# Fetching spilled results earlier, and making two of a pair's four weight sums by DMAs that add in place

## The chip, the cores and the metric

The kernel runs on one core of one Trainium2 chip. Its time is measured on the device, in microseconds (us). The engines that matter are TensorE (PE, the matmuls), VectorE (DVE), ScalarE (ACT), GpSimd (POOL, which here only issues DMAs) and SyncE (SP, which issues most DMAs).

## What is computed

Two layers of an encoder on 256 positions of 2048 channels, in float32. Cut to what matters here:

```python
h = rmsnorm(x, norm_w)
proj = h @ w_in          # q_m k_m v_m z_m o_m g_m q_r k_r v_r z_r gate_m gate_r
h_m = mlstm_scan(forward) + flip(mlstm_scan(backward))
u_m = head_rmsnorm(sigmoid(o_m) * h_m) * silu(z_m)
h_r = retention_scan(forward) + flip(retention_scan(backward))
u_r = head_rmsnorm(h_r) * silu(z_r)
mix = sigmoid(concat([gate_m, gate_r]) + b_mix)
y = mix[:, :2048] * (u_m @ w_proj_m) + mix[:, 2048:] * (u_r @ w_proj_r)
x = x + y @ w_out
```

After the second layer stands one more rmsnorm.

## The kernel before

Positions lie in two tiles of 128, contracted channels in 16 tiles of 128. A weight block is 2048 x 512. It is loaded from HBM in eight chunks of 128 x 1024 float32 (two contraction tiles side by side, 512 KB), each into a tile `raw` out of seven. To keep float32 accuracy every operand is split into a rounded part and a rest: ACT casts `raw` to `whi` (line 262), DVE subtracts to get `wlo` (line 263), and PE makes three matmuls for each product (lines 271 to 273: hi x hi, hi x lo of the weight, lo of the activation x hi). Twelve tiles hold `whi` and `wlo`, so at most six chunks are split ahead of PE.

`gemm` multiplies one block with both position tiles: 12 matmuls of 512 columns for each of its eight chunks. GEMMs follow one another in the order of the layer: qk, v_m (vm), q and k of the retention (qr), v_r (vr), z_m (zm), proj_m (pj), z_r (zr), proj_r (pj), w_out (wo).

Seven pairs of blocks (two of o_m, two of gate_m, one of z_r, two of gate_r) are not multiplied by `gemm`, but by `seven`, which needs seven half-size products for a pair of blocks in place of eight (the scheme of Strassen and Winograd, with four sums of weights). Its steps are items in a list with weights, and `gemm` runs as many of them behind each chunk as a running goal allows (`side_chunk`): "side work". For a column chunk i (0 to 3) of a pair, `p1` loads three chunks of weights, r11, r12 and r22, and multiplies r11; `p5` makes r11 + r12 (line 268, through `wsum`) and multiplies it; `p6` adds r22 to that, into the tile `keep` (line 445), and multiplies; `p7` makes r12 + r22 (line 268) and multiplies. After all four i, `middle` combines the products to one result, and `p2` to `p4` go over the lower half: two loads r21 and r22, products of each, and `p4`, which adds r21 to `keep` (line 268) and multiplies. `end` makes the other three results. So a column chunk has four sums on DVE, 56 of each kind in the whole run (7 pairs, 4 chunks, 2 layers).

Results that are needed later (hm, om, gm, hr, zr, gr, ym, y, x: 128 x 512 float32, 256 KB) go to HBM by `spill` (a DMA on POOL's queue, line 99) and come back by `fetch` (a DMA on SP's queue, line 105) into tiles of 512 columns, of which there are seven. `gated` is such a step beside the zm GEMMs: it fetches hm_b and so_b (the spilled hm and om), multiplies them on DVE and squares them on ACT.

Steps that run beside a GEMM are generators in a list `pending`; `run_later` advances the first of them by one `yield` behind each chunk, from chunk number `lead` on (3 unless given). The order of instructions on each engine is made by a scheduler from the order of the code and from priorities: `tc.high_priority(offset=n)` moves an instruction n instructions ahead of its place (AHEAD is 800, URGENT 1600), and `vec` and `sca` are DVE and ACT with URGENT (their rows all have line 119). Every engine and every queue takes its instructions in that order.

## Time and profile before

| what | value |
|---|---|
| median of three runs | 2194.8 us (2194.19 to 5458.12) |
| the profiled execution's own time | 2194.46 us |
| its span, first to last instruction | 2192.4 us |
| mean granted TensorE clock | 0.995 |
| PE busy | 2154.0 us, 98% |
| DVE busy | 1813.4 us, 83% |
| ACT busy | 1304.3 us, 59% |
| POOL busy | 66.9 us, 3% |
| moved by DMA | 518.25 MB, 236 GB/s on average |

Busy time is the union of an engine's instructions; a matmul's end is modelled, and matmuls overlap, so a busy PE can still be short of work for some tenths of a us at a time. The 5458.12 us is a single run far off the other two and is not used.

### The profile page before, as it was taken

Reading aid. Unit: us, or ns where it says so; the run is one execution under the profiler, and the core shown is the slowest. Engines: PE = TensorE matmul, PEld = TensorE weight load, DVE = VectorE, ACT = ScalarE, POOL = GpSimd, SP = SyncE. Lnnn points to the kernel's source line nnn. Section 1 sums busy time; section 2 is a strip of 40 time slices with the busy share of each in tenths; the row PEclk is TensorE's granted clock in tenths of the full one; section 3 lists DMA queues with packets and bytes.
Section 4 is the critical chain, followed back from the end, with each engine's and each line's share of the span. In section 5 each row is a group of like instructions: output and inputs, shape, how many; then the busy total and the mean of one; then the engine's idle time right before and its main releaser. Section 6 shows DMA issues by size and latency. Waiting matters only on the chain.

```text
span 2192.4 us, 28486 instructions
## 1 busy us (share of the span) xinstructions
PE 2154.0 (98%) x10024; PEld 1809.9 (83%) x10024; DVE 1813.4 (83%) x2327; ACT 1304.3 (59%) x1627; POOL 66.9 (3%) x130
## 2 busy tenths in 40 slices
PE   7999999999999999999999999999999999999998
PEld 7988888888778888888899888888887788888887
DVE  6997898897898998985578778989978989889854
ACT  6745466656775656564457555665567656565543
POOL 0000000000000000000000000000000000000000
PEclk9999999999999999999999999999999999999999
DMA  8645577767777887887656456776777778878963
GB/s 277 213 150 190 191 236 236 229 229 241 241 241 264 280 283 258 271 295 276 221 168 208 164 185 210 236 234 216 240 247 239 255 255 292 280 252 277 326 223 125
DMA packets 161071, 518.25 MB, mean 236 GB/s; under 512 B 19616, under 2 KB 22176, under 8 KB 160928
## 3 DMA queue, kind: packets, MB, share of 16 engines
q1 hardware_dynamic: 143552, 471.98, 65.4%
q0 software_dynamic: 9600, 31.46, 3.6%
q10 hardware_dynamic: 7776, 13.00, 2.0%
q8 instruction: 78, 1.28, 0.2%
q14 instruction: 65, 0.53, 0.1%
HBM read 482.81 MB, written 33.55 MB: 236 GB/s over the span
## 4 chain that ended last, share of the span: by engine, by line
issue 48%; PE 42%; DVE 3%; DMA 3%; POOL 2%; ACT 1%; SPq 0%; ACTq 0%; POOLq 0%; DVEq 0%
PE pj L272 3%; PE pj L273 3%; PE pj L271 3%; DVE wlo L263 2%; PE vm L271 1%; PE vm L272 1%; PE wo L273 1%; PE wo L272 1%; PE wo L271 1%; PE vr L271 1%; PE vr L272 1%; PE qr L271 1%; PE vm L273 1%; PE qr L273 1%; PE vr L273 1%
## 5 line engine op out<-in xcount | busy, mean ns | idle before, releaser
L262 ACT CAST whi<-raw 128x1024 fp32r<-128x1024 f32 (+2 forms) x832 | 844.6, 1034 | 608.1 <-DVE raw L268 147.7
L263 DVE TENSOR_TENSOR wlo<-raw,whi 128x1024 fp32r<-128x1024 f32 (+2 forms) x832 | 981.0, 1200 | 214.7 <-ACT whi L262 200.1
L272 PE MATMUL pj<-wlo,u_hi 128*128 128x512 f32 x512 | 199.4, 390 | 0.6 <-DVE wlo L263 0.5
L271 PE MATMUL pj<-whi,u_hi 128*128 128x512 f32 x512 | 199.9, 391 | 0.0
L273 PE MATMUL pj<-whi,u_lo 128*128 128x512 f32 x512 | 199.3, 389 | 0.0
L262 ACT CAST whi<-keep 128x1024 fp32r<-128x1024 f32 x112 | 117.7, 1051 | 60.0 <-PE qr L272 12.8
L263 DVE TENSOR_TENSOR wlo<-keep,whi 128x1024 fp32r<-128x1024 f32 x112 | 136.4, 1218 | 15.7 <-ACT whi L262 15.1
L268 DVE TENSOR_TENSOR raw<-raw 128x1024 f32<-128x1024 f32 x112 | 136.4, 1218 | 0.8
L271 PE MATMUL qk<-whi,ht_hi 128*128 128x384 f32 (+2 forms) x320 | 113.7, 357 | 10.5 <-ACT whi L262 10.5
L272 PE MATMUL qk<-wlo,ht_hi 128*128 128x384 f32 (+2 forms) x320 | 113.4, 354 | 1.0 <-DVE wlo L263 1.0
L272 PEld LDWEIGHTS pj<-wlo,u_hi 128*128 128x128 f32 x512 | 96.1, 188 | 21.0 <-DVE wlo L263 1.5
L273 PE MATMUL qk<-whi,ht_lo 128*128 128x384 f32 (+2 forms) x320 | 113.0, 353 | 0.0
L273 PEld LDWEIGHTS pj<-whi,u_lo 128*128 128x128 f32 x512 | 96.1, 188 | 20.0
L271 PEld LDWEIGHTS pj<-whi,u_hi 128*128 128x128 f32 x512 | 96.0, 188 | 20.0 <-ACT whi L262 0.4
L272 PE MATMUL zm<-wlo,ht_hi 128*128 128x512 f32 x256 | 100.0, 391 | 1.0 <-DVE wlo L263 0.9
L271 PE MATMUL vm<-whi,ht_hi 128*128 128x512 f32 x256 | 100.3, 392 | 0.0
L273 PE MATMUL vm<-whi,ht_lo 128*128 128x512 f32 x256 | 100.2, 391 | 0.0
L271 PE MATMUL vr<-whi,ht_hi 128*128 128x512 f32 x256 | 100.1, 391 | 0.0
L271 PE MATMUL qr<-whi,ht_hi 128*128 128x512 f32 x256 | 100.1, 391 | 0.0
L272 PE MATMUL vm<-wlo,ht_hi 128*128 128x512 f32 x256 | 100.0, 391 | 0.0
L271 PE MATMUL zm<-whi,ht_hi 128*128 128x512 f32 x256 | 100.0, 392 | 0.0
L272 PE MATMUL vr<-wlo,ht_hi 128*128 128x512 f32 x256 | 99.8, 390 | 0.0
(313 smaller groups left out, 4664.6 us busy)
## 6 DMA issues: line engine op xcount, KB each, us to landing
raw<-in_w_main_dram SPq DMA_DIRECT2D x776, 512.0 KB, 5.0
raw<-in_w_qk_dram SPq DMA_DIRECT2D x48, 384.0 KB, 3.2
bm<-in_b_mix_dram ACTq DMA_DIRECT2D x32, 256.0 KB, 4.4
raw<-in_w_qk_dram SPq DMA_DIRECT2D x15, 400.0 KB, 5.2
hm<-hm POOLq DMA_DIRECT2D x16, 256.0 KB, 4.6
om<-c POOLq DMA_DIRECT2D x16, 256.0 KB, 3.5
hr<-hr POOLq DMA_DIRECT2D x16, 256.0 KB, 5.7
gm<-c POOLq DMA_DIRECT2D x16, 256.0 KB, 4.7
```

What stands on the lines that cost most here:

```text
L262: nc.scalar.copy(out=whi, in_=raw)
L263: nc.vector.tensor_tensor(out=wlo, in0=raw, in1=whi.bitcast(F32), op=ALU.subtract)
L268: nc.vector.tensor_tensor(out=dst, in0=a, in1=b, op=ALU.add)
L271: nc.tensor.matmul(out=ps, lhsT=xh, rhs=whi, start=first, stop=False)
L272: nc.tensor.matmul(out=ps, lhsT=xh, rhs=wlo, start=False, stop=False)
L273: nc.tensor.matmul(out=ps, lhsT=xl, rhs=whi, start=False, stop=last)
```

## The change

Five edits, most of them in `seven`. `p1` loads its third chunk into a tile named t3 and then issues a DMA on POOL's queue (line 439 of the changed kernel) that adds r12 to it from HBM in place, so that t3 is r12 + r22. `p5` writes r11 + r12 over r12 and not over r11, `p6` adds r11 and t3 into `keep` (line 449), and `p7` multiplies t3 without a sum. After `p6` a second DMA on POOL's queue (line 452) adds r21 to `keep` from HBM, and `p4` loses its sum. The weights of the items p7 and p4 fall from 1.6 to 0.5. The bias rows `bm` are loaded by `early` in the last chunk of each half, on SP's queue in place of ACT's.

The fetches move: `gated` fetches all four tiles of a block at once and then pauses two slots, and the zm GEMMs run their later-steps from chunk 1 on; gm_b is fetched before its GEMM; `ur_chunk` fetches z_b like `gated`; ym_b (for b below 2) and gr_b (from 2 on) are fetched before their GEMM.

```diff
@@ -408,7 +408,7 @@
             yield
         side_start(make_items(s_hi=s_hi, s_lo=s_lo, keep=bigt("keep", 4)), 20 * NCK)
 
-    def seven(l, xop, s_hi, s_lo, keep, blk, finish):
+    def seven(l, xop, s_hi, s_lo, keep, blk, finish, early):
 
         def sop(i, kt):
             o = (i * HK + kt) * P
@@ -430,24 +430,29 @@
             if i == 0:
                 for name in "abcd":
                     st["ps_" + name] = bank("s" + name)
+            if i == HC - 1:
+                early(1)
             load("r11", 0, i)
             load("r12", 1, i)
-            load("r22", 1, HC + i)
+            load("t3", 1, HC + i)
+            with tc.high_priority(offset=AHEAD):
+                nc.gpsimd.dma_start(out=st["t3"], in_=wmain(l, blk + 1)(i), accum_op=ALU.add)
             product(st["ps_a"], lambda kt: xop(0, kt), st["r11"], i, True, True)
 
         def p5(i):
-            wsum(st["r11"], st["r11"], st["r12"])
-            product(st["ps_c"], lambda kt: sop(0, kt), st["r11"], i, True, True)
+            wsum(st["r12"], st["r11"], st["r12"])
+            product(st["ps_c"], lambda kt: sop(0, kt), st["r12"], i, True, True)
 
         def p6(i):
             with tc.high_priority(offset=AHEAD):
                 t2 = keep[:, i * CW:(i + 1) * CW]
-                nc.vector.tensor_tensor(out=t2, in0=st["r11"], in1=st["r22"], op=ALU.add)
+                nc.vector.tensor_tensor(out=t2, in0=st["r11"], in1=st["t3"], op=ALU.add)
             product(st["ps_b"], lambda kt: sop(1, kt), t2, i, True, True)
+            with tc.high_priority(offset=AHEAD):
+                nc.gpsimd.dma_start(out=t2, in_=wmain(l, blk)(HC + i), accum_op=ALU.add)
 
         def p7(i):
-            wsum(st["r12"], st["r12"], st["r22"])
-            product(st["ps_d"], lambda kt: sop(2, kt), st["r12"], i, True, True)
+            product(st["ps_d"], lambda kt: sop(2, kt), st["t3"], i, True, True)
 
         def middle():
             with tc.high_priority(offset=URGENT):
@@ -465,6 +470,8 @@
             if i == 0:
                 for name in "acd":
                     st["ps_" + name] = bank("r" + name)
+            if i == HC - 1:
+                early(0)
             load("r21", 0, HC + i)
             load("r22", 1, HC + i)
             product(st["ps_a"], lambda kt: xop(0, HK + kt), st["r21"], i, True, True)
@@ -474,7 +481,6 @@
 
         def p4(i):
             t2 = keep[:, i * CW:(i + 1) * CW]
-            wsum(t2, t2, st["r21"])
             product(st["ps_d"], lambda kt: xop(1, HK + kt), t2, i, True, True)
 
         def end():
@@ -490,11 +496,11 @@
 
         items = []
         for i in range(HC):
-            for w, fn in ((0.5, p1), (1.6, p5), (1.6, p6), (1.6, p7)):
+            for w, fn in ((0.5, p1), (1.6, p5), (1.6, p6), (0.5, p7)):
                 items.append((w, lambda fn=fn, i=i: fn(i)))
         items.append((2.0, middle))
         for i in range(HC):
-            for w, fn in ((0.5, p2), (0.5, p3), (1.6, p4)):
+            for w, fn in ((0.5, p2), (0.5, p3), (0.5, p4)):
                 items.append((w, lambda fn=fn, i=i: fn(i)))
         items.append((1.5, end))
         return items
@@ -818,25 +824,30 @@
 
         def side_items(l=l, xop=xop, rs=rs, s_hi=None, s_lo=None, keep=None):
             def finish_with(kind, b0):
+                bms = {}
+
+                def early(n):
+                    if kind in ("gm", "gr"):
+                        bms[n] = row("bm")
+                        mc = (0 if kind == "gm" else D) + (b0 + n) * NB
+                        nc.sync.dma_start(out=bms[n], in_=b_mix[l:l + 1, mc:mc + NB].broadcast_to([P, NB]))
+
                 def finish(t, n, src, own):
                     sg = t512(kind) if own is None else own
                     b = b0 + n
                     if kind in ("om", "zr"):
                         sca.activation(out=sg, in_=src, func=AF.Sigmoid if kind == "om" else AF.Silu, scale=rs[t])
                     else:
-                        bm = row("bm")
-                        mc = (0 if kind == "gm" else D) + b * NB
-                        with tc.high_priority(offset=AHEAD):
-                            nc.scalar.dma_start(out=bm, in_=b_mix[l:l + 1, mc:mc + NB].broadcast_to([P, NB]))
+                        bm = bms[n]
                         vec.scalar_tensor_tensor(out=sg, in0=src, scalar=rs[t], in1=bm, op0=ALU.mult,
                                                        op1=ALU.add)
                         sca.activation(out=sg, in_=sg, func=AF.Sigmoid)
                     spill((kind, l, b, t), sg)
-                return finish
+                return finish, early
             items = []
             for kind, base, b in (("om", B_O_M, 0), ("om", B_O_M, 2), ("gm", B_GATE, 0), ("gm", B_GATE, 2),
                                   ("zr", B_Z_R, 0), ("gr", B_GATE + NBLK, 0), ("gr", B_GATE + NBLK, 2)):
-                items += seven(l, xop, s_hi, s_lo, keep, base + b, finish_with(kind, b))
+                items += seven(l, xop, s_hi, s_lo, keep, base + b, *finish_with(kind, b))
             return items
 
         for b in range(NBLK):
@@ -892,9 +903,10 @@
         um = []
 
         def gated(h, hs, ss):
-            for t in range(NT):
-                hv = fetch(("hm", l, h, t), "hm_b")
-                so = fetch(("om", l, h, t), "so_b")
+            ops = [(fetch(("hm", l, h, t), "hm_b"), fetch(("om", l, h, t), "so_b")) for t in range(NT)]
+            yield from pause(2)
+            for t in range(NT):
+                hv, so = ops[t]
                 vec.tensor_tensor(out=hv, in0=hv, in1=so, op=ALU.mult)
                 sca.activation(out=so, in_=hv, func=AF.Square, accum_out=ss[:, t:t + 1])
                 hs.append(hv)
@@ -912,7 +924,7 @@
             hs = []
             ss_m = sm.tile([P, NT], F32, name="ss_m")
             later(gated, b, hs, ss_m)
-            ps = gemm(xop, wmain(l, B_Z_M + b), "zm")
+            ps = gemm(xop, wmain(l, B_Z_M + b), "zm", lead=1)
             while len(hs) <= NT:
                 run_later()
             rstd_m = hs[NT]
@@ -931,10 +943,12 @@
 
         uop = lambda t, kt: in_acts(um)(t, kt)
         for b in range(NBLK):
+            for t in range(NT):
+                side_need(("gm", l, b, t))
+            sgs = [fetch(("gm", l, b, t), "gm_b", 60) for t in range(NT)]
             ps = gemm(uop, wmain(l, B_PROJ_M + b), "pj")
             for t in range(NT):
-                side_need(("gm", l, b, t))
-                sg = fetch(("gm", l, b, t), "gm_b")
+                sg = sgs[t]
                 vec.tensor_tensor(out=sg, in0=ps[t], in1=sg, op=ALU.mult)
                 spill(("ym", l, b, t), sg)
 
@@ -943,16 +957,18 @@
         def ur_chunk(b, zs):
             ev = []
             hrs = [fetch(("hr", l, 2 * b + k), "hr_b") for k in range(2)]
-            for t in range(NT):
-                z = fetch(("zr", l, b, t), "z_b") if zs is None else zs[t]
+            if zs is None:
+                zs = [fetch(("zr", l, b, t), "z_b") for t in range(NT)]
+                yield from pause(2)
+            for t in range(NT):
+                z = zs[t]
                 for k in range(2):
                     i = t * NH_R + 2 * b + k
                     zk = z[:, k * S:(k + 1) * S]
                     vec.scalar_tensor_tensor(out=zk, in0=hrs[k][:, t * S:(t + 1) * S], scalar=rstd_r[:, i:i + 1],
                                              in1=zk, op0=ALU.mult, op1=ALU.mult)
                 ev.append(z)
-            if zs is None:
-                yield
+            yield
             ur[b] = transpose_split(ev, b, None, None, (l, V_RN))
             yield
 
@@ -987,12 +1003,18 @@
                 y_hi, y_lo = bigt("y_hi", 2, F32R), bigt("y_lo", 3, F32R)
                 later(y_chunk, None, 0)
                 later(y_chunk, None, 1)
+            early = []
+            for t in range(NT):
+                if b < 2:
+                    early.append(fetch(("ym", l, b, t), "ym_b", 60))
+                    continue
+                early.append(fetch(("gr", l, b, t), "gr_b", 60))
             ps = gemm(rop, wmain(l, B_PROJ_R + b), "pj", lead=2)
             ev = []
             for t in range(NT):
                 side_need(("gr", l, b, t))
-                sg = fetch(("gr", l, b, t), "gr_b")
-                ym = fetch(("ym", l, b, t), "ym_b")
+                sg = fetch(("gr", l, b, t), "gr_b") if b < 2 else early[t]
+                ym = fetch(("ym", l, b, t), "ym_b") if b >= 2 else early[t]
                 vec.tensor_tensor(out=sg, in0=ps[t], in1=sg, op=ALU.mult)
                 vec.tensor_tensor(out=sg, in0=ym, in1=sg, op=ALU.add)
                 ev.append(sg)
```

The order of instructions changes with it. Three places:

DVE, the second pair of o_m, its first column chunk. Here raw_4119 is r11, raw_4121 is r12 and raw_4123 is r22 before and t3 now; keep_2236 is `keep`. Before:

```order
L263 TENSOR_TENSOR wlo_4126<-raw_4119,whi_4125 128x1024
L119 TENSOR_TENSOR c21_4084<-rd_3783,u7_3752 128x512
L263 TENSOR_TENSOR wlo_4152<-raw_4149,whi_4151 128x1024
L268 TENSOR_TENSOR raw_4119<-raw_4119,raw_4121 128x1024
L445 TENSOR_TENSOR keep_2236<-raw_4119,raw_4123 128x1024
L263 TENSOR_TENSOR wlo_4169<-raw_4119,whi_4168 128x1024
L263 TENSOR_TENSOR wlo_4181<-raw_4178,whi_4180 128x1024
L263 TENSOR_TENSOR wlo_4198<-keep_2236,whi_4197 128x1024
L263 TENSOR_TENSOR wlo_4210<-raw_4207,whi_4209 128x1024
L119 TENSOR_TENSOR qr_lo_4032<-tr_4135,qr_hi_4031 128x512
L119 TENSOR_TENSOR qr_lo_4032<-tr_4142,qr_hi_4031 128x512
L268 TENSOR_TENSOR raw_4121<-raw_4121,raw_4123 128x1024
```

Now, from the split that frees the tile of raw_4121 (wlo_3969) over the one that frees the tile of raw_4123 (wlo_3999) to the add into keep:

```order
L263 TENSOR_TENSOR wlo_3969<-raw_3966,whi_3968 128x1024
L263 TENSOR_TENSOR wlo_3985<-keep_2236,whi_3984 128x1024
L263 TENSOR_TENSOR wlo_3999<-raw_3994,whi_3998 128x1024
L268 TENSOR_TENSOR raw_4121<-raw_4119,raw_4121 128x1024
L263 TENSOR_TENSOR wlo_4009<-raw_3996,whi_4008 128x1024
L263 TENSOR_TENSOR wlo_4039<-raw_4036,whi_4038 128x1024
L263 TENSOR_TENSOR wlo_4055<-keep_2236,whi_4054 128x1024
L119 SCALAR_TENSOR_TENSOR ca_4018<-qr0_3695,rstd_328,cos_sb_103 128x512
L119 SCALAR_TENSOR_TENSOR sa_4019<-qr0_3695,rstd_328,sin_sb_104 128x512
L449 TENSOR_TENSOR keep_2236<-raw_4119,raw_4123 128x1024
```

The sum of r12 and the add into keep stood next to each other and behind the split of r11; now both stand ahead of r11's split (which follows twelve rows later), with three splits and two other rows between them.

DVE, the second block of `gated` in layer 0: the rows from the z rows of the first block (they read its hm_b) to the second product of the second. c11 to c21 are the results of a pair of gate_m, u_lo is the split of u. Before:

```order
L119 SCALAR_TENSOR_TENSOR z_5045<-hm_b_5022,rstd_m_5034,z_5045 128x512
L119 SCALAR_TENSOR_TENSOR z_5048<-hm_b_5028,rstd_m_5034,z_5048 128x512
L263 TENSOR_TENSOR wlo_5221<-raw_5218,whi_5220 128x1024
L119 SCALAR_TENSOR_TENSOR c21_5074<-c21_5074,rstd_328,bm_5090 128x512
L119 SCALAR_TENSOR_TENSOR u_lo_5175<-tr_5176,vec_sb_101,u_hi_5174 128x256
L119 SCALAR_TENSOR_TENSOR u_lo_5175<-tr_5185,vec_sb_101,u_hi_5174 128x256
L119 TENSOR_TENSOR hm_b_5212<-hm_b_5212,so_b_5214 128x512
L119 TENSOR_TENSOR hm_b_5263<-hm_b_5263,so_b_5265 128x512
L119 SCALAR_TENSOR_TENSOR u_lo_5175<-tr_5176,vec_sb_101,u_hi_5174 128x256
L119 SCALAR_TENSOR_TENSOR u_lo_5175<-tr_5185,vec_sb_101,u_hi_5174 128x256
L263 TENSOR_TENSOR wlo_5238<-raw_5102,whi_5237 128x1024
```

Now:

```order
L119 SCALAR_TENSOR_TENSOR z_5050<-hm_b_4956,rstd_m_5036,z_5050 128x512
L119 SCALAR_TENSOR_TENSOR z_5047<-hm_b_4952,rstd_m_5036,z_5047 128x512
L119 SCALAR_TENSOR_TENSOR c11_5074<-c11_5074,rstd_328,bm_4978 128x512
L119 SCALAR_TENSOR_TENSOR c12_5075<-c12_5075,rstd_328,bm_4519 128x512
L119 SCALAR_TENSOR_TENSOR c21_5076<-c21_5076,rstd_328,bm_4978 128x512
L263 TENSOR_TENSOR wlo_5179<-raw_5136,whi_5178 128x1024
L119 TENSOR_TENSOR hm_b_5151<-hm_b_5151,so_b_5153 128x512
L268 TENSOR_TENSOR raw_5250<-raw_5248,raw_5250 128x1024
L119 SCALAR_TENSOR_TENSOR u_lo_5093<-tr_5094,vec_sb_101,u_hi_5092 128x256
L119 SCALAR_TENSOR_TENSOR u_lo_5093<-tr_5103,vec_sb_101,u_hi_5092 128x256
L119 TENSOR_TENSOR hm_b_5155<-hm_b_5155,so_b_5157 128x512
L263 TENSOR_TENSOR wlo_5191<-raw_5188,whi_5190 128x1024
```

The products moved by a row or two; three rows c stand between z and the first product where one stood, and the sum of r12 stands between the two products.

POOL, the second pair of o_m beside the retention's spills (hr). Before:

```order
L99 DMA om_0_0_1_3113<-c21_3102 128x512
L99 DMA hr_0_0_3259<-hr_3254 128x512
L99 DMA hr_0_1_3324<-hr_3319 128x512
L99 DMA hr_0_2_3606<-hr_3601 128x512
L99 DMA hr_0_3_3655<-hr_3650 128x512
L99 DMA om_0_3_1_3761<-c22_3754 128x512
L99 DMA om_0_2_0_4089<-c11_4082 128x512
L99 DMA om_0_3_0_4092<-c12_4083 128x512
L99 DMA om_0_2_1_4095<-c21_4084 128x512
```

Now:

```order
L439 DMA raw_3295<-in_w_main_dram 128x1024
L452 DMA keep_2236<-in_w_main_dram 128x1024
L99 DMA hr_0_0_3249<-hr_3244 128x512
L439 DMA raw_3445<-in_w_main_dram 128x1024
L452 DMA keep_2236<-in_w_main_dram 128x1024
L99 DMA hr_0_1_3326<-hr_3321 128x512
L439 DMA raw_3617<-in_w_main_dram 128x1024
L452 DMA keep_2236<-in_w_main_dram 128x1024
L99 DMA hr_0_2_3593<-hr_3588 128x512
```

An accumulation into t3 (raw) and one into keep now stand between two spills, and t3 of the next chunk ahead of keep of this one.

## Rows read from the trace of the kernel before

**Rows 1.** The page, part 1: busy time, share, instructions of each engine.

```profile
PE 2154.0 (98%) x10024; PEld 1809.9 (83%) x10024; DVE 1813.4 (83%) x2327; ACT 1304.3 (59%) x1627; POOL 66.9 (3%) x130
```

**Rows 2.** Timeline of PE, 573.3 to 580.5: start, length, engine, line, idle before.

```profile
573.62 0.39 PE L273 MATMUL zm<-whi,ht_lo 128*128 128x512 f32 x1
573.85 0.39 PE L271 MATMUL sd<-whi,s_hi 128*128 128x512 f32 x1
578.85 0.79 PE L272 MATMUL sd<-wlo,s_hi 128*128 128x512 f32 x1 [4.61 <-DVE wlo L263]
579.44 0.63 PE L273 MATMUL sd<-whi,s_lo 128*128 128x512 f32 x1
579.87 0.63 PE L271 MATMUL sd<-whi,s_hi 128*128 128x512 f32 x1
```

**Rows 3.** Table of stretches: length, busy of each engine, clock, DMA share, GB/s.

```profile
0.00:55.00 55.00, 43.46 (x217) 41.27 (x218) 34.68 (x77) 36.86 (x66) 1.68 (x10) 0.94 0.80 276
...
220.00:990.00 770.00, 762.65 (x3472) 633.08 (x3471) 674.01 (x730) 473.12 (x556) 27.13 (x50) 1.00 0.75 250
550.00:660.00 110.00, 102.92 (x457) 83.98 (x457) 95.77 (x131) 79.81 (x108) 2.71 (x5) 0.97 0.73 243
...
1330.00:2090.00 760.00, 752.06 (x3427) 622.11 (x3426) 666.55 (x726) 468.13 (x551) 26.05 (x48) 1.00 0.77 257
1650.00:1760.00 110.00, 102.72 (x454) 82.19 (x452) 97.12 (x127) 78.00 (x100) 3.25 (x6) 1.00 0.74 247
...
2145.00:2192.40 47.40, 38.96 (x218) 34.04 (x216) 18.58 (x37) 13.49 (x25) 0.00 (x0) 0.95 0.29 104
```

**Rows 4.** View of waits, whole run: engine, releaser, us, times, longest.

```profile
DVE wlo L263 <- ACT whi L262: 215.2, 189, 4.9
...
ACT whi L262 <- PE vm L272: 84.7, 49, 5.9
...
DVE keep L268 <- DMA raw<-in_w_main_dram: 34.0, 21, 5.1
...
DVE hm_b L119 <- DMA so_b<-om: 19.4, 11, 3.3
...
DVE c L119 <- DMA bm<-in_b_mix_dram: 8.2, 2, 4.3
...
DVE z L119 <- DMA hr_b<-hr: 7.3, 4, 2.1
...
DVE gm_b L119 <- DMA gm_b<-gm: 5.7, 2, 2.9
```

**Rows 5.** Timeline of DVE, 563.3 to 579.

```profile
569.12 0.75 DVE L119 SCALAR_TENSOR_TENSOR c<-c,rstd,bm 128x512 f32<-128x512 f32 x1
...
573.37 0.69 DVE L119 TENSOR_TENSOR hm_b<-hm_b,so_b 128x512 f32<-128x512 f32 x1 [2.72 <-DMA so_b<-om]
576.18 0.69 DVE L119 TENSOR_TENSOR hm_b<-hm_b,so_b 128x512 f32<-128x512 f32 x1 [2.12 <-DMA so_b<-om]
...
577.58 1.21 DVE L263 TENSOR_TENSOR wlo<-raw,whi 128x1024 fp32r<-128x1024 f32 x1
```

**Rows 6.** Groups of instructions of DVE by shape: count, busy, mean ns.

```profile
L268 DVE TENSOR_TENSOR raw<-raw 128x1024 f32<-128x1024 f32 x112 | 136.4, 1218 | 0.8
```

**Rows 7.** Timeline of DVE, 710 to 720: four splits in a row.

```profile
712.29 4.63 DVE L263 TENSOR_TENSOR wlo<-raw,whi 128x1024 fp32r<-128x1024 f32 x4 [1.19 <-ACT whi L262]
```

**Rows 8.** DMA view: queues, then issues with KB and us to landing.

```profile
q1 hardware_dynamic: 143552, 471.98, 65.4%
...
raw<-in_w_main_dram SPq DMA_DIRECT2D x776, 512.0 KB, 5.0
...
hm<-hm POOLq DMA_DIRECT2D x16, 256.0 KB, 4.6
...
so_b<-om SPq DMA_DIRECT2D x16, 256.0 KB, 6.1
```

**Rows 9.** Groups of instructions of POOL.

```profile
L99 POOL DMA_DIRECT2D hm<-hm x16 | 8.8, 552 | 440.4 <-ACT hm L119 440.2 <-ACT cos_sb L210 0.2
```

## Prediction

> **What bounds the kernel now.** I read the busy times first. TensorE (PE) is busy in 2154.0 of 2192.4 us, VectorE (DVE) in 1813.4 [rows 1]. A busy PE is not proof that it gives work without a break, so the timeline is next: each 512-column matmul is shown as 0.39 us long, but the next one starts 0.23 us later (573.62, 573.85) [rows 2]. The 0.23 is the pace of a fed PE. Right behind it stands a break: the next matmul starts at 578.85, and for a while afterwards the pace is 0.43 us (579.44, 579.87). The granted clock in 550:660 has a mean of 0.97, so some 3.3 us more are lost after that wait at the lower of the two levels (1.2 in place of 2.4 GHz) [rows 3].
>
> The table of stretches says where the 38.4 us lie in which PE isn't busy (2192.4 less 2154.0): 11.5 in the first 55 us, 8.4 in the last 47.4, 7.1 in 550:660 and 7.3 in 1650:1760 [rows 3]. The middle has 18.4 in all, 14.4 of them in those two stretches, which are the same place of the two layers (the z_m GEMMs). With the 3.3 us of clock, 21.7 us is everything that the change can touch; start and end are outside of it. That is 1.0% of 2194.46 us, and about 2% is what a measurement of this kernel can tell from no change.
>
> Who makes PE wait there? The wait at 578.85 ended with DVE's split (line 263) [rows 2]. DVE had come to it late: two products hm_b*so_b stood ahead of it, each held by the landing of so_b, 2.72 and 2.12 us [rows 5]. In the whole run DVE waits 19.4 us for so_b, 8.2 for bm, 7.3 for hr_b, 5.7 for gm_b, and 34.0 us for weights at the sum into keep (line 268, 21 times); the 215.2 us behind ScalarE's cast I count as room, since that cast itself often waits for PE to free a pair of split tiles (84.7 us behind the vm GEMMs alone) [rows 4]. So DVE is the second limit: in the two side stretches (220:990, 1330:2090), where the pairs' products run beside the GEMMs, it is busy 674.0 of 770 and 666.6 of 760 us and idle 96.0 + 93.5 = 189.5 [rows 3].
>
> **The change part by part.**
>
> *Two sums leave DVE.* The sums in p7 and p4 go, 56 each (4 column chunks, 7 pairs, 2 layers). One is shown as 1.218 us, but four splits in a row take 4.63 us, so one costs DVE 1.157 [rows 6, 7]. 112 x 1.157 = 129.6 us of DVE time are removed, and the 34.0 us of waits at p4's sum with them. PE gains nothing from this by itself: it is room.
>
> *Fetches ahead.* hm_b/so_b are asked for two slots earlier, gm_b before its GEMM, bm a chunk earlier and on SP instead of ScalarE. A slot holds 12 matmuls of a GEMM, 12 x 0.23 = 2.7 us, and about one side product of 6, so two slots are some 8 us, against 6.1 us that so_b takes from issue to landing [rows 8]. By that the waits named above (19.4 + 8.2 + 7.3 + 5.7 = 40.6) should go. But a fetch also needs a tile. The one that made PE wait is the second block's in both layers, and there hm_b_5151 and so_b_5153 lie, in the new program, in the tiles that hm_b_4956 and hm_b_4952 had: their fetch waits for the two z rows that read these last. From the second z to the first product stand three rows c and one split, 3 x 0.7 + 1.2 = 3.3 us [rows 5, 7], against a landing of 6.1: DVE waits 2.8 us, as before (2.72) [rows 5]. Between the two products it now has a sum and two rows u_lo, some 2 us, that before came elsewhere, so of the second wait (2.12) little should be left. So in that block I count on half, in the other three on most. The bm DMAs on SP, and the fetches that wait there for a tile, hold the weight loads behind them; seven loads are on the way by then, and that covers it as long as the wait stays below two chunks (5.4 us).
>
> *112 accumulating DMAs on POOL.* A POOL DMA occupies the engine for 0.55 us [rows 9], 62 us in all on an engine that is otherwise 3% busy [rows 1]: nothing. While such a DMA waits on POOL (t3's for its load, keep's for the split that reads the tile), the spills behind it wait too, for a load of 5 us or so; their fetches come tens of us later, so only the tiles that they free are late. For the 16 DMA engines each is at least another 512 KB load; the SP queue moved 471.98 MB in 65.4% of the span, so one load takes 1.59 us of all engines, 112 take 178 us, or 356 if the add reads both operands at that price [rows 8]. The side stretches show a DMA share of 0.75 and 0.77 [rows 3]; 178 to 356 us over 1530 make that 0.88 to 1.00. The lower end is hidden, the upper one isn't.
>
> *Two new waits on DVE.* Here is the cost that decides. In the new order the sum of r12 no longer overwrites r11, so it stands as soon as its load is expected, and the add into keep stands as soon as the accumulated t3 is expected. DVE takes its work in order: while it waits for one of these, ready splits queue behind it, and PE waits for those. In the place shown, the tile of r12 is freed by split 3969 and its sum follows two splits later: 2.3 us, where a load takes 5.0 from issue to landing [rows 8]. t3's tile is freed by split 3999; until the add into keep there are four such rows and two of 0.75 us [rows 5], 6.1 us in all, for a load and an accumulation behind each other. I counted this for all 56 pairs, with the durations of [rows 7] and a load of 5.1 us. The r12 sums: short in 44 of 56 pairs, 115 us together. The same counting for the old sum into keep gives 33 us over 26 of 56, where the trace has 34.0 over 21 [rows 4], so I trust it. The adds depend on X, the time from issue to landing of an accumulation, which no row shows. A plain 512 KB load lands in 5.0 us and is the lower bound; the upper bound is two of them in series, 10 us; 256 KB written from POOL land in 4.6 [rows 8]. I take 6.6, the load and 1.6 us for the second operand, nearest to the load's row. The adds then wait 94 us in all at X = 5.0, 168 at 6.6, 208 at 7.4, 238 at 8 and 348 at 10.
>
> The Trainium skill, page "DMA: Bandwidth & Descriptors", section "Anatomy of one DMA", fits a DMA issued from GpSimd as 2.0 us and the bytes at 436 GB/s. For 512 KB that is an estimate of 3.2 us, by which the adds would wait 22 us in place of 168; the row of plain loads, 5.0, doesn't support it for SP's queue, and no row shows one of 512 KB on POOL's.
>
> *The sum for DVE.* Room: 189.5 idle + 129.6 removed = 319 us. New waits at X = 6.6: 115 + 168 = 283. It fits, with 36 us to spare, but only as an average. Before, the waits and the sums together were 129.6 + 34.0 + 40.6 = 204; now it is 283, so DVE isn't freed, it has changed one load for another. In a z_m stretch of 110 us: 9.7 us of so_b waits go (half of 19.4) and 9.3 us of sums (64.8 x 110/770); 20.2 us of new waits come (141.5 x 110/770). That is even. What speaks for a gain in spite of it: the old waits came together (2.72, 2.12 and a GEMM's end within 10 us), the new ones are spread over the pairs, and the add stands 5 to 26 rows of DVE ahead of the split that PE needs. Of the 21.7 us the second block has 4.6 and 3.3 of clock here, and about 4.6 in the other layer (where the mean clock is 1.00): 12.5, of which half goes with the second product's wait, 6.3. The other 9.2 are gaps that I let stay, since DVE's account is even. 3 us come for places where a new wait meets a PE without a lead: 2194.5 - 6.3 + 3 = **2191 us**. Span and the time around it differ by 2.1 us (2194.46 less 2192.4), the median of the runs is 2194.8; I predict against the 2194.46.
>
> **The rivals.**
>
> *DVE blocks on the accumulations (slower).* Same place, the add into keep, with a later landing. The room of 319 less 115 is 204 us, which is X = 7.4: from there on DVE cannot do its work in the side stretches, and PE waits for each missing us. X = 8 gives 353 us of waits, 34 over the room: 2191 + 34 = 2225. X = 10 gives 463, 144 over: 2335. For it: a DMA share that goes to 0.88 or more slows loads too, and the shortfalls are in nearly every pair. Against it: DVE's idle time behind the cast shows that it usually has a lead over PE.
> The skill, same page, section "Queues, rings and completion order", says that a DMA engine takes turns between its queues packet by packet; by that a load beside an accumulation would lose up to the 1.6 us of one transfer, and if all 44 short r12 sums lost that, it would be 70 us more, 36 of which the spare room takes: 2191 + 34 = 2225 again. No row shows what such an overlap costs.
>
> *The accumulations land early.* At X = 4.6, the row of POOL's 256 KB, the adds wait 76 us, all new waits are 191, 13 us less than the 204 that go, and 18.4 + 3.3 us are won but for 2: 2175. For it: that row itself, should the second half of the bytes cost little. The skill's fit above lies on this side.
>
> *The fetches aren't earlier.* The 512-column tiles have seven buffers; four are now asked for at once by a block's hm_b and so_b, two by gm_b or gr_b, three by a pair's results. If SP has to wait for a tile in all blocks as it does in the second, the fetches land as late as now and the weights behind them as well: the change then does not do what it says, and with the DVE account even the time is 2195. For it: the second block. Against it: in the third and fourth block the tiles that the new program gives to the first product come free before the z rows of the block ahead.
>
> **How the numbers follow.** The forecast 0.40 (2185 to 2197 by itself), DVE blocked 0.37, early 0.15, no earlier fetch 0.08. Of the 0.37 I put 0.12 beyond 2% (2238, X near 8.25) and 0.25 below. Slower by over 2%: 0.12; faster by over 2%: 0.01, since all that can be won is 21.7 us; within: 0.87. The range goes from 2172 (all of the 21.7 but the last us) to 2234 (X near 8.2), which leaves some 0.13 above and 0.04 below.
>
> **What the changed profile would show.** PE without a wait of several us in 550:660 and 1650:1760, and a granted clock of 1.00 there: fetches right; one near 3 us at the second block's products: the tile rule above. DVE's waits: the row hm_b <- so_b gone or under 5 us, and new rows for raw (r12's sum) near 115 us and keep (the add) near 170 behind a DMA; if the latter is under 80, the early rival, if over 210, the slow one. The DMA view gives X directly. I'd be wrong above all if X is far from 6.6, or if PE in the z_m stretches doesn't stand a wait of 5 us of DVE at once.

## The result, and the profile after

The changed kernel takes 2446.32 us (median of 4 runs), the kernel before 2194.49: 1.1153 times as long, 95% interval 1.1131 to 1.1175 (the one run of 5458.12 us is left out of the ratio). The forecast was 2191 us, 2172 to 2234. The time lies 212 us above the range.

The page of the profiled execution (2447.13 us, span 2445.4, granted clock 0.960), part 1, answers to [rows 1]:

```profile
PE 2234.1 (91%) x10024; PEld 1850.7 (76%) x10024; DVE 1686.7 (69%) x2215; ACT 1293.7 (53%) x1621; POOL 166.8 (7%) x242
```

PE is without work for 211.3 us (2445.4 less 2234.1) where it was 38.4, and it is busy 80.1 us longer for the same 10024 matmuls, which goes with the lower clock (0.960 after 0.995). 172.9 + 80.1 = 253.0, the whole difference of the spans. DVE does 126.7 us less work, as two sums of four should give, and yet it is idle 758.7 us in place of 379.0.

The view of waits over the whole run, which answers to [rows 4] (engine, line, what it waited for; us in total, times, longest):

```profile
DVE keep L449 <- DMA raw<-in_w_main_dram: 301.7, 51, 9.7
POOL keep L452 <- DVE wlo L263: 256.2, 45, 16.1
...
DVE wlo L263 <- ACT whi L262: 197.4, 177, 4.2
ACT whi L262 <- DMA raw<-in_w_main_dram: 178.0, 59, 9.7
...
DVE raw L268 <- DMA raw<-in_w_main_dram: 126.5, 44, 6.5
...
PE pj L272 <- DVE wlo L263: 66.1, 20, 8.5
```

Two rows are new on DVE: 301.7 us at the add into keep (line 449) and 126.5 us at the sum of r12, 428.2 together; the 34.0 us at the old sum into keep are gone. The wait behind ScalarE's cast is there as before, 197.4 after 215.2. ScalarE's own wait for weights was smaller before:

```profile
ACT whi L262 <- DMA raw<-in_w_main_dram: 34.2, 21, 5.0
```

So DVE's account closes: +394.2 at the sums, -17.8 at the cast, -126.7 of work, which is 249.7 of the 253.0 us.

One such place in DVE's timeline, from 229 us on (start, length, engine and line, idle before it and what ended that):

```profile
229.19 1.21 DVE L263 TENSOR_TENSOR wlo<-raw,whi 128x1024 fp32r<-128x1024 f32 x1
232.50 1.23 DVE L268 TENSOR_TENSOR raw<-raw 128x1024 f32<-128x1024 f32 x1 [2.10 <-DMA raw<-in_w_main_dram]
233.64 2.35 DVE L263 TENSOR_TENSOR wlo<-raw,whi 128x1024 fp32r<-128x1024 f32 x2
244.56 1.23 DVE L449 TENSOR_TENSOR keep<-raw 128x1024 f32<-128x1024 f32 x1 [8.56 <-DMA raw<-in_w_main_dram]
245.70 1.22 DVE L263 TENSOR_TENSOR wlo<-keep,whi 128x1024 fp32r<-128x1024 f32 x1
246.84 4.62 DVE L263 TENSOR_TENSOR wlo<-raw,whi 128x1024 fp32r<-128x1024 f32 x4
...
257.20 1.22 DVE L268 TENSOR_TENSOR raw<-raw 128x1024 f32<-128x1024 f32 x1 [4.43 <-DMA raw<-in_w_main_dram]
...
260.34 1.21 DVE L263 TENSOR_TENSOR wlo<-raw,whi 128x1024 fp32r<-128x1024 f32 x1
```

DVE stands 2.10 us before the sum of r12 and 8.56 before the add, although splits are ready: five of them run behind it without a pause. Then the next chunk's sum of r12 stops it for 4.43 us, and the split at 260.34 is the one that PE waits for, in its own timeline:

```profile
256.40 0.39 PE L271 MATMUL sc<-whi,s_hi 128*128 128x512 f32 x1
261.61 0.50 PE L272 MATMUL sc<-wlo,s_hi 128*128 128x512 f32 x1 [4.82 <-DVE wlo L263]
...
262.23 0.63 PE L271 MATMUL sc<-whi,s_hi 128*128 128x512 f32 x1
262.66 0.63 PE L272 MATMUL sc<-wlo,s_hi 128*128 128x512 f32 x1
```

PE stands for 4.82 us, and goes on at a step of 0.43 us, the lower of the two levels (1.2 in place of 2.4 GHz), where a fed PE has 0.23 [rows 2].

The DMA view, which answers to [rows 8] (queue: packets, MB, share of the 16 engines; then KB and median us from issue to landing):

```profile
q0 software_dynamic: 25728, 90.19, 16.3%
...
raw<-in_w_main_dram SPq DMA_DIRECT2D x776, 512.0 KB, 5.6
raw<-in_w_main_dram POOLq DMA_DIRECT2D x56, 512.0 KB, 8.8
keep<-in_w_main_dram POOLq DMA_DIRECT2D x56, 512.0 KB, 9.2
```

An accumulation lands 8.8 or 9.2 us after its issue. The forecast had put 6.6, between 5 and 10.

### The profile page after: what moved, and what is told of

Its sections match the earlier page's. It is cut to its first block, busy times and chain, and to the rows that moved or that the text cites. A ratio compares the mean times of both kernels' runs of the same rounds, so it can differ in the third digit from the quotient of the medians.

```text
span 2445.4 us, 28722 instructions
## 1 busy us (share of the span) xinstructions
PE 2234.1 (91%) x10024; PEld 1850.7 (76%) x10024; DVE 1686.7 (69%) x2215; ACT 1293.7 (53%) x1621; POOL 166.8 (7%) x242
## 3 DMA queue, kind: packets, MB, share of 16 engines
q0 software_dynamic: 25728, 90.19, 16.3%
## 5 line engine op out<-in xcount | busy, mean ns | idle before, releaser
L262 ACT CAST whi<-raw 128x1024 fp32r<-128x1024 f32 (+2 forms) x832 | 847.6, 1034 | 706.6 <-DMA raw<-in_w_main_dram 178.0
L449 DVE TENSOR_TENSOR keep<-raw 128x1024 f32<-128x1024 f32 x56 | 68.6, 1224 | 301.7 <-DMA raw<-in_w_main_dram 301.7
L272 PE MATMUL pj<-wlo,u_hi 128*128 128x512 f32 x512 | 214.0, 418 | 66.1 <-DVE wlo L263 66.1
L273 PE MATMUL pj<-whi,u_lo 128*128 128x512 f32 x512 | 210.3, 411 | 0.0
L271 PE MATMUL pj<-whi,u_hi 128*128 128x512 f32 x512 | 209.9, 410 | 0.0
L272 PEld LDWEIGHTS pj<-wlo,u_hi 128*128 128x128 f32 x512 | 102.4, 200 | 96.7 <-DVE wlo L263 75.7
L268 DVE TENSOR_TENSOR raw<-raw 128x1024 f32<-128x1024 f32 x56 | 68.5, 1224 | 131.7 <-DMA raw<-in_w_main_dram 126.5
L273 PEld LDWEIGHTS pj<-whi,u_lo 128*128 128x128 f32 x512 | 103.0, 201 | 21.3
L272 PE MATMUL qr<-wlo,ht_hi 128*128 128x512 f32 x256 | 103.1, 403 | 13.9 <-DVE wlo L263 13.9
L439 POOL DMA_DIRECT2D raw<-in_w_main_dram x56 | 49.1, 877 | 837.6 <-DMA raw<-in_w_main_dram 242.3
L273 PE MATMUL vr<-whi,ht_lo 128*128 128x512 f32 x256 | 102.5, 400 | 0.0
```

The costliest lines, as they stand in the source:

```text
L262: nc.scalar.copy(out=whi, in_=raw)
L268: nc.vector.tensor_tensor(out=dst, in0=a, in1=b, op=ALU.add)
L271: nc.tensor.matmul(out=ps, lhsT=xh, rhs=whi, start=first, stop=False)
L272: nc.tensor.matmul(out=ps, lhsT=xh, rhs=wlo, start=False, stop=False)
L273: nc.tensor.matmul(out=ps, lhsT=xl, rhs=whi, start=False, stop=last)
L439: nc.gpsimd.dma_start(out=st["t3"], in_=wmain(l, blk + 1)(i), accum_op=ALU.add)
```

## The experiments

Theory A: DVE takes its instructions in order, and in the changed kernel two of them stand so early that their data hasn't landed; ready splits queue behind, and PE with them. Theory B: the 112 extra DMAs themselves, on the DMA engines and on POOL's queue, make everything late. Theory C: the moved fetches hold the weights back. All ratios are to the kernel before, on the same chip.

| run | median us | ratio, 95% interval | waits for DMAs at the sums on DVE, us |
|---|---|---|---|
| 1 fetches only | 2205.64 | 1.0053, 1.0039 to 1.0067 | 23.6 |
| 2 keep's accumulation only | 2217.80 | 1.0107, 1.0093 to 1.0121 | none |
| 3 t3's accumulation only | 2442.64 | 1.1135, 1.1115 to 1.1154 | 451.2 |
| 4 add doesn't read t3 | 2251.41 | 1.0258, 1.0244 to 1.0272 | 156.0 |
| 5 sums in their old place | 2218.32 | 1.0127, 1.0108 to 1.0146 | 107.5 |
| 6 copies, no additions | 2312.37 | 1.0532, 1.0507 to 1.0558 | 303.1 |
| 7 all DMAs, nothing on DVE waits | 2216.59 | 1.0105, 1.0090 to 1.0121 | none |
| 8 some of the fetches | 2193.80 | 1.0009, 1.0000 to 1.0018 | 22.6 |
| 9 accumulate behind the add | 2299.01 | 1.0476, 1.0461 to 1.0492 | none |
| 10 t3 loaded first | 2355.72 | 1.0736, 1.0719 to 1.0753 | 291.2 |
| 11 keep's accumulation, some fetches | 2209.14 | 1.0073, 1.0059 to 1.0087 | none |
| 12 early sums, no accumulation | 2227.58 | 1.0147, 1.0128 to 1.0166 | 160.0 |

**1, fetches only.** p5 to p7 and p4 as before the change.

> The changed kernel with its fetches and its early bias rows, and with the four sums of a pair on DVE as before, so without the 112 accumulating DMAs. Theory A (DVE stands in order behind sums whose loads and accumulations have not landed; 301.7 us at the add into keep and 126.5 us at the sum of r12 in the changed kernel) and theory B (the 112 extra DMAs load the DMA engines and the POOL queue, and everything comes later) both expect the time of before less what the fetches give: 2180 to 2195 us. Theory C (the fetches asked for earlier hold the weight loads behind them on SP's queue: ScalarE waited 178.0 us for weights, 34.2 before) expects 2250 or more. The wait of hm_b for so_b (19.4 us before) should be 8 to 12 us, as in the changed kernel (12.0).

12 us slower, a little above A and B, far from C. The wait of hm_b for so_b is 19.2 us, not the 8 to 12 expected: the earlier fetches did not shorten it. The z_m stretch gained nothing and the y chunk lost; PE's waits:

```profile
PE tr L235 <- DMA y_b<-y: 5.4, 2, 3.3
PE tr L235 <- DVE z L119: 4.9, 2, 2.8
```

Before, the first of these rows had 0.2 us and the second 0.4.

**2, keep's accumulation only.**

```diff
-            load("t3", 1, HC + i)
-            with tc.high_priority(offset=AHEAD):
-                nc.gpsimd.dma_start(out=st["t3"], ..., accum_op=ALU.add)
+            load("r22", 1, HC + i)
```

(and p5 to p7 as before the change)

> The changed kernel with one accumulation alone: r21 into keep (56 DMAs); r12 + r22 is a DVE sum again, and the sums stand in the order of before. Nothing on DVE waits for an accumulation. Theory A expects no new wait on DVE, the 34.0 us at the old sum into keep gone, and 2180 to 2195 us. Theory B expects about half of the 252 us that the change costs: 2300 to 2340 us. A POOL queue that holds spills back behind an accumulation that waits would lie between, 2200 to 2260.

24 us, above A's range and in that of the last case; 12 of them are those of the fetches. Half of the accumulations cost a twentieth of what the change costs: B falls.

**3, t3's accumulation only.** Line 452 out, p4's sum back on DVE.

> The changed kernel with the other accumulation alone: r12 into t3 (56 DMAs), and the sum into keep on DVE again. Counted on the order of DVE with a load of 5.6 and an accumulation of 9.0 us from issue to landing, the sums wait 206 us (r12 and keep) and the adds 345 us, 551 together against some 475 in the changed kernel by the same count. Theory A expects it as slow as the changed kernel or slower: 2430 to 2510 us. Theory B expects half of the cost: 2300 to 2340 us.

As slow as the whole change, with half of its DMAs. The waits are those of A:

```profile
DVE keep L449 <- DMA raw<-in_w_main_dram: 261.2, 52, 8.2
...
DVE keep L268 <- DMA raw<-in_w_main_dram: 105.1, 40, 4.4
DVE raw L268 <- DMA raw<-in_w_main_dram: 84.9, 30, 4.6
```

**4, the add doesn't read t3.**

```diff
-                nc.vector.tensor_tensor(out=t2, in0=st["r11"], in1=st["t3"], op=ALU.add)
+                nc.vector.tensor_tensor(out=t2, in0=st["r11"], in1=st["r12"], op=ALU.add)
```

> The changed kernel, both accumulations issued as there, but the add into keep (line 449) reads r12 in place of t3, so that it waits for no accumulation; t3 is read by its own split alone. The values of this product are other ones, the instructions the same in number and size. Theory A expects the 301.7 us at the add gone, some 123 us left at the sum of r12, and at the rate of the changed kernel (252 us for 428 us of waits, 0.59) 2194 + 0.59 x 123 = 2267 us, 2220 to 2300. Theory B expects the time of the changed kernel, 2420 to 2450, since all DMAs are there.

One operand of 56 adds takes back 195 of 252 us, with every DMA in place. The adds stand no later for it: counted in the traces, 13.5 rows of DVE ahead of the split of their result in the median, 11 in the changed kernel, 4 before. The 156.0 us that are left stand at the sum of r12:

```profile
DVE raw L268 <- DMA raw<-in_w_main_dram: 156.0, 46, 10.2
```

**5, the sums in their old place.**

```diff
-            wsum(st["r12"], st["r11"], st["r12"])
-            product(..., st["r12"], i, True, True)
+            wsum(st["r11"], st["r11"], st["r12"])
+            product(..., st["r11"], i, True, True)
```

> The changed kernel, but p5 writes r11 + r12 over r11 again and p6 adds t3 to that, so that both sums stand behind the split of r11, where they stood before the change (the median add stands 4 rows ahead of the split that needs it, in place of 10.5). Every DMA is there and the add still waits for t3's accumulation; r12 goes into keep twice, so the values are other ones. Counted as for the changed kernel (load 5.6, accumulation 9.0 us): no wait at the sum of r12, 175 us over 44 adds, against 475. Theory A, from the runs so far (156 us of such waits cost 58 us, 428 cost 252, so 0.7 us for each beyond some 75): 2194 + 0.7 x 100 = 2264, 2235 to 2300. If the place of the sums is not what matters, but that DVE waits for an accumulation at all: 2380 or more.

Below the range expected: 228 us come back, though the add still waits for the accumulation. DVE's waits:

```profile
DVE wlo L263 <- ACT whi L262: 267.7, 240, 4.2
DVE keep L449 <- DMA raw<-in_w_main_dram: 107.5, 33, 7.1
```

The landing is no shorter (9.0 us for t3); but behind the split of r11 most of it has passed, and the 107.5 us that remain (33 times) cost next to nothing, run 7 without any is 1.7 us faster. The median add stands 4 rows ahead of the split of its result again. That is the sharpest of the twelve: same DMAs, same dependence on t3, another place in DVE's queue.

**6, copies in place of additions.** `accum_op` left out at both DMAs.

> The changed kernel with the 112 DMAs of POOL's queue as plain copies over the tile, not additions, in the same places and with the same waits; t3 is then r12 and keep r21, so the values are other ones. It measures what the addition costs. If the time from issue to landing (8.8 and 9.2 us) comes from the addition, it falls to 5 to 6 us, the adds wait 154 us by the count in place of 337, and the time is near 2194 + 0.7 x (154 + 138 - 75) = 2346, 2300 to 2390. If it comes from the queue and from the weights beside it, landing stays at 8 us or more and the time within 2% of the changed kernel.

The DMA view and DVE's waits:

```profile
q0 software_dynamic: 25728, 90.19, 11.1%
...
raw<-in_w_main_dram POOLq DMA_DIRECT2D x56, 512.0 KB, 6.2
keep<-in_w_main_dram POOLq DMA_DIRECT2D x56, 512.0 KB, 7.1
```

```profile
DVE wlo L263 <- ACT whi L262: 191.8, 175, 4.2
DVE keep L449 <- DMA raw<-in_w_main_dram: 182.9, 50, 7.9
DVE raw L268 <- DMA raw<-in_w_main_dram: 120.2, 42, 5.4
```

The addition itself adds 2.6 and 2.1 us to the landing, 125 us to the waits and 134 us to the time. Without it the change would still cost 118 us. The time lies in the range of the first case, the landing a little above its 5 to 6 us.

**7, all DMAs, nothing on DVE waits.** Runs 4 and 5 together: p5 as in 5, and p6 adds r12 to r11.

> All 112 accumulations issued as in the changed kernel, but no sum on DVE waits for one: p5 writes r11 + r12 over r11 as before the change, p6 adds r12 to that in place of t3, and t3 and keep are read by their own splits alone. Values of these products are other ones. What remains is the load on the DMA engines and on POOL. Theory A: 56 of these DMAs cost 12 us (keep alone against fetches alone, 2217.8 and 2205.6), 112 cost 24: 2230 us, 2210 to 2250. Theory B would have most of the 252 us remain.

11 us above the fetches alone: the price of 112 accumulations on the DMA engines and on POOL. The lower weights of the items p7 and p4 are in this run and in run 5 as well, so theirs lies within the same few us. The side stretch 220:990 (length; busy time of PE, PEld, DVE, ACT, POOL; clock, DMA share, GB/s) is as full as in any run, 0.91 where it was 0.75 [rows 3], and PE is as busy there as before, but for 4 us:

```profile
220.00:990.00 770.00, 758.78 (x3441) 628.83 (x3440) 615.21 (x670) 471.63 (x550) 76.44 (x105) 1.00 0.91 287
```

**8, some of the fetches.** Run 1 with ym_b and gr_b fetched where they were before.

> The fetches of the change alone, as in the first experiment (2205.6 us), but ym_b and gr_b are fetched where they were before the change. In the run of all fetches PE waited 5.4 us for y_b (not at all before), and 8.1 and 4.8 us were idle in 550:660 and 1650:1760, as before (7.1 and 7.3). If the loss of 12 us is the y chunk's, the time is 2192 to 2198; if it is in the z_m stage and elsewhere, 2202 to 2208.

No different from before by its interval (2 us above): nearly all of the 12 us were the y chunk's. In run 1 gr_b's fetches stand ahead of y_b's on SP's queue in both layers, and wait there for the spill of gr to land (at 969.07 in layer 0, at 2058.41 and 2062.06 in layer 1); y_b is asked for behind them:

```profile
2062.07 0.33 SPq L105 DMA_DIRECT2D gr_b<-gr  x1
2062.50 1.80 SPq L105 DMA_DIRECT2D y_b<-y  x4
```

In run 8 gr_b isn't ahead, and y_b is asked for at 2048.30. PE's wait for y_b is 0.4 us there; the one for z (4.5) stays and costs nothing to be seen. The whole run's wait of hm_b for so_b is 20.0 us after 19.4. In the second z_m block of layer 0 the waits are shorter than the 2.72 and 2.12 of [rows 5], but not gone:

```profile
567.29 0.69 DVE L119 TENSOR_TENSOR hm_b<-hm_b,so_b 128x512 f32<-128x512 f32 x1 [1.24 <-DMA so_b<-om]
569.81 0.69 DVE L119 TENSOR_TENSOR hm_b<-hm_b,so_b 128x512 f32<-128x512 f32 x1 [1.82 <-DMA so_b<-om]
```

**9, accumulate behind the add.** A version that computes the right products and takes both sums from DVE: r22 is loaded and added as before the change, then POOL adds r12 to its tile for p7.

```diff
+                nc.vector.tensor_tensor(out=t2, in0=st["r11"], in1=st["r22"], op=ALU.add)
+            with tc.high_priority(offset=AHEAD):
+                nc.gpsimd.dma_start(out=st["r22"], in_=wmain(l, blk + 1)(i), accum_op=ALU.add)
```

> Both sums leave DVE, with no DVE wait for an accumulation and the reference's values: r22 is loaded and added into keep as before the change, and only then does POOL's DMA add r12 to it for p7; keep gets r21 by a DMA as in the changed kernel. Sums stand where they stood before the change. The fetches are those of the run of some fetches (2193.8 us). Counted: no wait at any sum. What is left is the price of the 112 DMAs: 11 us between all DMAs without DVE waits (2216.6) and the fetches alone (2205.6). Theory A: 2194 + 11 = 2205, 2196 to 2212. If freeing DVE (129.6 us of sums, 34 of waits) gives PE something: below 2190. If adding after DVE has read the tile only moves the wait to ScalarE's cast of r22: 2230 or more.

A's number is wrong by 94 us. The last of the three cases came true: the cast of that tile is the next that needs it, and ScalarE takes its work in order as well.

```profile
DVE wlo L263 <- ACT whi L262: 465.0, 237, 8.6
...
ACT whi L262 <- DMA raw<-in_w_main_dram: 319.3, 72, 9.5
```

Of ScalarE's 319.3 us (34.2 before) 291.2, in 50 waits, are for these accumulations and 28.2 for plain loads; DVE waits 465.0 behind ScalarE, and PE behind both.

**10, t3 loaded first.** The load of t3 and its accumulation ahead of the loads of r11 and r12.

> The changed kernel with the loads of p1 in another order: t3 and its accumulation ahead of r11 and r12. If the wait is that of a load and an accumulation in series, a start two loads earlier should take 2 to 5 us from each of the 56 adds: 2300 to 2350. But the add's place on DVE moves with its load, and counted on the new order the adds wait 313 us (337 in the changed kernel) and the sums of r12 62 (138): 374 in place of 475, 0.79 of the wait, so 2194 + 0.7 x (0.79 x 428 - 75) = 2378, 2355 to 2400.

91 us better than the change, at the lower end of what the count on DVE's order gave: the waits are 291.2 us, 0.68 of 428.2.

**11, keep's accumulation with some fetches.** Run 2 with the fetches of run 8.

> The accumulation into keep alone (56 DMAs) with the fetches of the run of some fetches, that is without the earlier ym_b and gr_b. With all fetches it took 2217.8 us, 12 more than the fetches alone. If these 12 are the DMAs' own, the sum is 2193.8 + 12 = 2206 (2200 to 2210); if they are only y_b, which lands late behind the earlier fetches (PE waited 12.7 us for it there, 5.4 with the fetches alone), 2192 to 2198.

15 us above run 8: these are the DMAs' own, not the y chunk's. They don't go by the count of DMAs (56 cost as much as the 112 of run 7, which also takes twice as many sums off DVE). Loads land in 5.4 us in place of 5.0, and ScalarE waits 90.7 us for weights (44.5 in run 8); which of the two makes it, no run separates.

**12, early sums without any accumulation.**

```diff
-            wsum(st["r11"], st["r11"], st["r12"])
+            wsum(st["r12"], st["r11"], st["r12"])
...
-            wsum(st["r12"], st["r12"], st["r22"])
+            wsum(st["r22"], st["r12"], st["r22"])
```

> No accumulating DMA at all, four sums on DVE, the fetches of the run of some fetches (2193.8 us), but p5 writes r11 + r12 over r12 as in the changed kernel, so that the sum of r12 and the add into keep lose their order behind the split of r11 and move ahead (p6 adds r22 to r11, p7 adds r22 to the tile of r12: other values, the same instructions). It separates the place of the sums from the accumulations. Counted with a load of 5.1 us: 141 us of waits at the sums and 6 at the adds, 34 at the sums before. By the rate of the runs so far, 0.7 us for each beyond some 75: 2194 + 0.7 x 72 = 2244, 2220 to 2290 (DVE keeps its 129.6 us of sums here, which speaks for the upper end). If only waits for accumulations cost, below 2205.

34 us above run 8, with no accumulating DMA at all: the place of the sums costs by itself, even for plain loads. The waits at the sums grew by 137 us over run 8, and DVE's wait at the cast fell from 228.4 to 151.0, so that part of them was paid from there.

```profile
DVE wlo L263 <- ACT whi L262: 151.0, 138, 4.2
DVE raw L268 <- DMA raw<-in_w_main_dram: 81.7, 34, 6.6
DVE keep L268 <- DMA raw<-in_w_main_dram: 72.7, 34, 4.9
```

No version beat the kernel before; run 8 is equal to it.

## Why the prediction was wrong

*What held.* The mechanism that the forecast called "the cost that decides", and its place, the add into keep. The count on DVE's order gave 115 us at the r12 sums (measured 126.5). With the landing as it then was, between the counts for X = 8 (238) and X = 10 (348) lie the measured 301.7. The work removed: 126.7 of 129.6 us. The DMA engines: 112 plain copies were put at 178 us of all engines; in run 6 they took 11.1% of 2311.1 less 3.6% of 2192.4 = 178 us, and the accumulations 16.3% of 2445.4 less the same 79 = 320, in the range up to 356. Their cover held too (11 us, run 7). POOL was put at 62 us for them and had 100; what that cost is within the 11 us. The rival by which a load beside an accumulation is late, with 70 us more at the sums of r12, didn't come: they have 126.5 after a count of 115, and loads land in 5.6 us after 5.0.

*The step that failed: the room.* "Room: 189.5 idle + 129.6 removed = 319 us" took all of DVE's idle time in the side stretches as free, that behind the cast too, so that 283 us of waits would fit and each us beyond would cost one. Run 6 is that very case: 6.2 and 7.1 us of landing, 303.1 us of waits, under the 319. It took 2312 us and not 2191. The sum had a term for this, "3 us come for places where a new wait meets a PE without a lead"; in run 6 it is 95 to 106 us (118 less the 12 of the fetches, and less up to 11 for the DMAs themselves).

Where did the room stay? Of the 215.2 us at the cast 128.7 lie outside of the parts in which the pairs run (232:965 and 1314:2049 before), and in the changed kernel 129.5 of 197.4 (outside of 229:1087 and 1439:2295); the sum, made of the side stretches, didn't count them. Inside it was 86.5 us before, and is 67.9 in the changed kernel and 60.5 in run 6: most of the idle time there stayed idle, while PE waited elsewhere in the same parts. So in these two the waits used hardly more than the work that left: 428.2 - 34.0 - 126.7 = 267.5 us, against 253.0 measured, and 142 in run 6 (126.9 us of work left there) for 118. But that is no law. In run 3 (69.9 us of work left) it gives 347 for 248, in run 12 (7.2) 119 for 34, in run 4 nothing for 57. In runs 3 and 12 the wait at the cast inside the pairs' parts falls to 9.3 and 23.2 us, so there most of it did serve as room. What decides how much of it serves, no run here separates.

Why so much of it didn't serve in the changed kernel was read from the traces, not tested by a run. The idle time lies where DVE is ahead: 163.1 of the 215.2 us stand behind a cast that had itself waited for PE to give tiles back. The waits come in large pieces instead: in the place shown 8.56 and 4.43 us with 8 us of work between them, and PE comes to the end of its split tiles behind the second. Behind it the raw tiles come free late and loads are asked for late (SP's queue waits 1637.4 us for splits after 1402.2), and ScalarE's own waits for weights rise from 34.2 to 178.0 us. The cause of DVE's wait at the cast is no other than before: 162.0 of the 197.4 us stand behind a cast that had waited for PE, 9.5 behind one that had waited for weights. The forecast's sentence against this rival, that the idle time behind the cast "shows that it usually has a lead", was by this a wrong reading: a lead on average, while the waits at the add come as single pieces of 6 us (301.7 over 51).

*The term that was mis-sized: X.* 6.6 was taken as a load and the time of a second operand. 8.8 and 9.2 were measured; that is worth 134 us (run 6 against the change; run 6 also takes 142 us of work off the DMA engines, and run 7 bounds what that is worth at 11). So of the 252 us over the kernel before, 118 come at about the landing that the forecast had put (6.2 and 7.1 us for its 6.6), and 134 from X. The rival "DVE blocks" had the right mechanism and gave 2225 at X = 8 and 2335 at X = 10; its price, from the same room, was as wrong as the forecast's.

The Trainium skill, page "DMA: Bandwidth & Descriptors", section "Anatomy of one DMA", gives by its fit an estimate of 3.2 us for 512 KB from GpSimd. The trace doesn't agree: plain copies on that queue landed in 3.9 us at the least and 6.2 or 7.1 in the median, beside the weights (run 6). The same page of the Trainium skill, section "Rules for kernel authors", says that an accumulating DMA reads its destination and writes it later; the 2.6 and 2.1 us between runs with and without the addition agree with a second pass of that kind.

*The fetches.* They were to give 6.3 us; they cost 12 (run 1), all but 2 of it in the y chunk (run 8). The forecast's rival of 0.08 had fetches wait for tiles; what held y_b back was its place on SP's queue, behind a fetch of gr_b that waited for gr. The waits for bm and gm_b (8.2 and 5.7 us) went, that for so_b didn't: 20.0 us in run 8 where 19.4 were to become 9.7. It is 12.0 in the changed kernel, where DVE is late itself. In the second z_m block of run 8, 1.24 and 1.82 us of wait remain where 2.8 and almost nothing were forecast; that the sum over both products fits (3.1) is luck, for their division doesn't, and in the other layer they are 1.27 and 3.05. PE is idle there as before, 7.3 and 6.1 us in 550:660 and 1650:1760 of run 8 against 7.1 and 7.3 [rows 3], so that these waits had not been all that it lacked.

## What to carry to other kernels

Work that leaves an engine is worth nothing if an instruction that needs a transfer stays on it in an earlier place: in a queue that is taken in order, ask for each waiting instruction what stands ready behind it, and for how long at once. Don't count an engine's idle time as room for its waits: in run 6 all waits together were less than the room, and it cost 118 us. How much of the idle time paid differed from run to run, of the 86.5 us at the cast beside the pairs the change used 18.6 and run 3 77.2, so a sum over averages can't tell; two waits of 8 and 4 us close to each other can end a lead that the average has. Where two operands of a chain become one transfer behind another, look for the place in the consumer's order first; here the same DMAs cost 252 us or some 25, by the place of two sums in DVE's queue (the change, run 5).

## What the runs showed of the hardware

A DMA that adds into SBUF took POOL 0.88 and 0.92 us in the mean, against 0.55 for a plain one [rows 9]; landed 8.8 and 9.2 us after its issue (11.1 for keep in run 5), 5.5 at the least, where the plain copy of the same 512 KB took 6.2 and 7.1, 3.9 at the least; and took 2.9 us of all 16 DMA engines (320 us over 112) where the copy took 1.6 (178 over 112). With a DMA share of 0.91 and 0.90 in the side stretches (run 7) the time rose by 11 us only over the fetches alone.
